# Attention's gates through DRAM: gating one token tile at a time instead of one column block of four tiles

## The chip, the cores and the metric

One core of one Trainium2 chip. The metric is the device time of one launch in microseconds (us), as the median of several runs. The engines are TensorE (PE; PEld is its weight load), VectorE (DVE), ScalarE (ACT), GpSimd (POOL) and the DMA queue that SyncE (SP) issues. [...]

## The reference, cut to what matters

Two layers over 1024 tokens of width 1024. In each layer one input projection feeds three groups of heads: sliding-window attention, retention and gated linear attention. Only the first is touched here.

```
s = einsum('bnqhgd,bnkhd->bnhgqk', qb, kk) * (D ** -0.5)      # 128 queries against 256 keys
p = softmax(concatenate([where(valid, s, -1e30), sink], -1))[..., :-1]
a_out = einsum('bnhgqk,bnkhd->bnqhgd', p, vv) * silu(ag)       # ag: the gate, a projection of h
y = concatenate([a_out, r_out, g_out], -1) @ w_out
x = x + gate * rms_norm(y, post_gain)
```

The attention has 8 query heads of width 64, two key heads, blocks of 128 tokens.

## The kernel before, in words

**Tiles.** The 1024 tokens are 8 tiles t of 128. Products that need full precision are made of two float32r halves: a tile is split into hi (a rounded copy) and lo (the rest), and three passes are summed, hi by hi, lo by hi, hi by lo (`PASSES`).

**Who sets the order.** The program is written as generators. `clk` is an estimate of PE's time that each matmul moves on; `job` puts a generator into a list, `pump` takes the jobs that are due forward between matmuls, a job says with `yield` how long it wants to wait (the table `L`, by names such as aq1 or ag1) or for which flag. So PE's order is the order in which matmuls are written under this clock, and it is kept. For the other engines and SP a scheduler orders the instructions when the kernel is built, by its own estimate of what is ready; a table `EN` picks the engine of many of them. Buffers are taken from pools by tag: `t2` is 10 buffers of 128x512, `t1` 7 of 128x256, `st` 5 for weights; PSUM has 8 banks, 3 for projections (`mm`) and 5 for the rest (`aux`).

**Attention.** `attn_run` starts one `attn_q` for each tile. A tile goes through these steps:
1. its queries are split into `qs` (hi on ACT, L841, lo on DVE, L842). `qs` has a tag of its own with one buffer;
2. 24 score matmuls into four `aux` banks (12 in tile 0 are smaller). Their first two use hi as weights, the next two lo;
3. ACT copies the previous block's scores out (L934, seen as L150 smx<-aux), DVE the current block's under a mask (L935), DVE takes the maximum (L937), ACT the eight exponentials with their sums (L940), DVE the reciprocal (L943), POOL the normalising product `pn` (L945), DVE the 32x32 transposes (L947), POOL four products `pr` that fix the window's edge (L956);
4. 80 small matmuls with the values (PV) into four `aux` banks, and four copies out into `ao`, alternately ACT and DVE (L978, seen as L150 and L152 t<-aux);
5. `ao` is stored to DRAM (`aoS`).

In PE's order the scores of tile t+1 stand before PV of tile t, with some 40 matmuls of the gates' projection (or of the output product) between each two.

**Gates.** In `layer`, for each half hf of the tokens (four tiles) and each of four column blocks k, `project_T` makes the gate of 128 columns by 512 tokens; the job `gate` (L1617) makes it silu-like (tanh on ACT, L1620, a product on DVE, L1621), keeps it in a `t2` buffer, and waits until all four tiles' attention is done. It then reads block k of the four tiles back from `aoS` (L1625), multiplies (L1627), splits the result (`mg` and `mgl`, both DVE, L1638 and L1639), and stores hi and lo to `mixS`, in the last layer also the whole to `mixF`. Only then do the four tiles' flags `mix1` come.

**After that.** The output product reads a tile's `mixS` (`load_mix`). The last layer works on pairs of tiles from tile 2 on (`Pair`): it reads both tiles' `mixF`, forms sums and differences on DVE (L1338 to L1341), and adds products up (L1378). Each of its product waits for one of three `mm` banks, which DVE or ACT must have read out. In layer 0 the next layer's normalisation (`pre`) follows each finished tile: DVE scales (L669), PE transposes.

Of the kernel before, what the change touches and what calls it, by code (L numbers as in the profile page):

```python
# [94 lines left out]
def trunk(ctx: ExitStack, tc: tile.TileContext, ins, cst, out):  # L95
# [88 lines left out]
    def lat(key, l):  # L184

        return L[key + "@1"] if l and key + "@1" in L else L[key]

# [3 lines left out]
    def flag(name, lat=0.0):  # L191
        flags[name] = clk[0] + lat
# [68 lines left out]
    mixF = dr.tile([NT, P, KT, P], F32, name="mixF")  # L261
    aoS = dr.tile([NT, P, 4, P], F32, name="aoS")
    vS = dr.tile([NT, P, P], F32, name="vS")
    sgS = dr.tile([NT, P, 256], F32, name="sgS")
    srS = dr.tile([NT, P, 256], F32, name="srS")
    tabS = dr.tile([NP_, P, 2, 256], F32, name="tabS")
# [573 lines left out]
    def split(hi, lo, src):  # L840
        A.activation(hi, src, AF.Copy)  # L841
        V.tensor_tensor(lo, src, f(hi), ALU.subtract)  # L842

    def attn_kv(l, t, pk):
        kr = t1()[:, 0:P]
        v = t1()[:, 0:P]
# [59 lines left out]

    def attn_q(l, t, q):

        qs = gp.tile([P, 2, 4, P], F32R, tag="qs", name=nm("qs"), bufs=1)
        split(qs[:, 0], qs[:, 1], q[:, :, P * (t % 4):P * (t % 4) + P])  # L910
        sm = gp.tile([P, 8, 129], F32, tag="smx", name=nm("smx"), bufs=SMB)
        V.tensor_copy(sm[:, :, 128], sink8[:, l])
        if t == 0:
# [5 lines left out]
        for g in range(2):  # L919
            for j in range(2):  # L920
                for i, (a, b) in enumerate(PASSES):
                    for r in range(2):
                        rr = slice(64 * r, 64 * r + 64)
                        mult(pss[g][r][:, j * n:(j + 1) * n], qs[rr, a, 2 * g + j], kv["kT"][b][rr, cols],
                             i == 0, i == 2, n / 4600.0)
        flag(("sc", l, t))
        if t % 4 == 3:
# [20 lines left out]
        cur, prev = kv[("v", t // 2)], kv.get(("v", max(t - 1, 0) // 2))  # L948
        tc_, tp = t % 2, (t - 1) % 2
        if t > 0:  # L950
            vd = gp.tile([P, P], F32, tag="vd", name=nm("vd"), bufs=1)
            G.tensor_tensor(vd, cur[:, 8 + tc_], prev[:, 8 + tp], ALU.subtract)
            pr = gp.tile([P, 8, 32], F32, tag="pr", name=nm("pr"), bufs=1)
            for i in range(4):
                rr = slice(32 * i, 32 * i + 32)
                eng(f"pr{i}").tensor_tensor(pr[rr], pb[rr, :, i, :], dmask[rr].unsqueeze(1).to_broadcast((32, 8, 32)),  # L956
                                            ALU.mult)
# [541 lines left out]
    def layer(l):  # L1499
# [111 lines left out]
        load(l, "ag0")  # L1611
        mx = {}

        def rows(d, hf, *i):
            return d[(slice(4 * hf, 4 * hf + 4), slice(None)) + i].rearrange("t p q -> p t q")

        def gate(g, hf, kk, pm):  # L1617
            k = 2 * g + kk
            th = t2()
            A.activation(th, pm, AF.Tanh, scale=0.5)  # L1620
            V.scalar_tensor_tensor(th, th, 1.0, pm, ALU.add, ALU.mult)  # L1621
            for t in range(4 * hf, 4 * hf + 4):
                yield (0.0, ("ao", l, t, g))
            ao = t2()
            dma("lao", ao.rearrange("p (t q) -> p t q", t=4), rows(aoS, hf, k))  # L1625
            yield lat("ag1", l)
            V.scalar_tensor_tensor(ao, th, 0.5, ao, ALU.mult, ALU.mult)  # L1627
            mh, ml = t2(F32R), t2(F32R)
            def tiles(x, ts):
                return x.rearrange("p (t q) -> p t q", t=4)[:, ts]  # L1630

            ts = slice(0, 4)
            if l == DEPTH - 1:
                t0 = max(PLAIN - 4 * hf, 0)
                if t0 < 4:
                    dma("sm0", rows(mixF, hf, k)[:, t0:4], tiles(ao, slice(t0, 4)))
                ts = slice(0, min(t0 + 1, 4)) if t0 else slice(0, 4, 2)
            copy("mg", tiles(mh, ts), tiles(ao, ts))  # L1638
            eng("mgl").tensor_tensor(tiles(ml, ts), tiles(ao, ts), tiles(f(mh), ts), ALU.subtract)  # L1639
            for a, m in ((0, mh), (1, ml)):  # L1640
                dma(f"sm{a}", rows(mixS, hf, a, k)[:, ts], tiles(f(m), ts))
# [65 lines left out]
        pump()  # L1707


B2, B1, BS, BST, MMB, SMB = 10, 7, 11, 5, 3, 3  # L1710
EN = {"shw0": "V", "shw1": "A", "shw2": "A", "shw3": "A", "slw0": "V", "slw1": "G", "slw2": "V", "slw3": "G", "sht2": "A", "sht3": "A", "sht4": "A", "slt2": "V", "slt3": "G", "slt4": "G", "sd": "V", "mh0": "A", "mh1": "A", "mh2": "A", "mh3": "A", "mf": "A", "ms0": "V", "ms1": "V", "ms2": "V", "ms3": "V", "yg0": "V", "yg1": "V", "ml0": "V", "ml1": "V", "ml2": "V", "ml3": "V", "mod0": "A", "mod1": "V", "qst": "S", "sv": "S", "lv": "S", "pr0": "G", "pr1": "G", "pr2": "G", "pr3": "G", "smh": "S", "sml": "S", "sm0": "S", "sm1": "S", "lao": "S", "sao": "S", "lmix": "S", "ssg": "S", "lsg": "S", "ssr": "S", "lsr": "S", "lx": "S", "sx": "A", "lw": "S", "lwm": "S", "whi0": "V", "whi1": "A", "whi2": "A", "whi3": "A", "wlo0": "V", "wlo1": "V", "wlo2": "V", "wlo3": "G", "xn0": "V", "xn1": "V", "hlo0": "V", "hlo1": "V", "rot0": "V", "rot1": "V", "rdec": "V", "kslo": "V", "qslo": "V", "vlo": "G", "kT": "A", "qT": "A", "sprev": "A", "pn": "G", "pf0": "A", "aoc0": "A", "aoc1": "V", "hng": "V", "mh": "A", "gso": "V", "mg": "V", "mgl": "V", "rT": "A", "rv": "A", "gv": "A", "gk": "A", "ak0": "V", "ak1": "V", "ak2": "V", "ak3": "V", "kd0": "G", "kd1": "G", "kd2": "G", "kx1": "G", "kx2": "G", "kx3": "V", "kx4": "V", "qb": "G", "stx": "V"}
L = {"sw1": 0.4, "ld1": 1.2, "ld2": 1.2, "ld1@1": 1.2, "ld2@1": 1.27, "swW00": 0.0, "swT1": 0.0, "swW11": 0.4, "swW10": 0.5, "tt1": 8.0, "tt2": 1.75, "tb1": 24.5, "tb2": 0.75, "pf3": 13.2, "pf1": 6.35, "pf2": 4.16, "mod1": 4.6, "mod2": 4.0, "mod3": 13.29, "mod4": 7.04, "mod5": 3.36, "mod6": 9.04, "pre1": 7.44, "kv1": 3.1, "kv2": 2.11, "aq1": 11.0, "aq7": 6.0, "ag1": 5.44, "aq2": 2.6, "aq6": 7.0, "aq3": 10.21, "aq4": 17.0, "aq5": 3.6, "hn1": 8.93, "hn2": 2.85, "gz1": 11.18, "gz2": 8.13, "gl1": 2.76, "gd3": 15.9, "gc1": 0.62, "gc2": 1.94, "gc3": 1.33, "gc4": 0.87, "gc6": 0.86, "gc5": 1.14, "rc1": 0.8, "rc2": 1.09, "rc3": 5.87, "rc4": 2.51, "fin1": 7.28, "lay1": 1.13, "gc4@1": 0.93, "mod2@1": 4.0, "mod3@1": 15.1, "mod5@1": 3.36, "mod6@1": 4.11, "pre1@1": 7.44, "kv1@1": 2.79, "kv2@1": 5.28, "aq1@1": 11.0, "aq7@1": 5.28, "ag1@1": 6.25, "aq2@1": 2.6, "aq6@1": 7.0, "aq3@1": 10.9, "aq4@1": 17.0, "aq5@1": 3.6, "hn1@1": 8.12, "hn2@1": 2.85, "gz1@1": 15.91, "gz2@1": 10.94, "gl1@1": 4.6, "gd3@1": 15.9, "gc1@1": 0.48, "gc2@1": 1.94, "gc3@1": 1.33, "gc6@1": 0.86, "gc5@1": 1.04, "rc1@1": 0.37, "rc2@1": 0.84, "rc3@1": 1.9, "rc4@1": 2.79, "fin1@1": 4.28, "lay1@1": 1.7}
CHUNK = 7
LAG = 2
FIN = 1
# [40 lines left out]
```

## Time and profile before

| | |
|---|---|
| runs, us | 1062.22, 1052.66, 1060.84; median 1060.84 |
| profiled execution, us | 1055.4, span 1053.6, mean granted clock 0.959 |
| PE busy | 968.1 us, 92% |
| PEld busy | 837.9 us, 80% |
| DVE busy | 703.8 us, 67% |
| ACT busy | 386.0 us, 37% |
| POOL busy | 259.7 us, 25% |
| DMA | 155.19 MB, mean 147 GB/s |
| attention's scores, layer 0 and layer 1 | from 328 to 437 us and from 830 to 944 us of the span |

Read the span as a queue of matmuls with holes. PE's order is fixed, so a hole is an instruction that waited, and the profile names what it waited for last. The holes' sizes are rows of the waits of PE and of PE's timeline (start, length, engine, line, operation, tile, count, and in brackets the idle time before it with its releaser); the other engines' timelines show why the releaser was late.

### The profile page before, as it was taken

What the parts mean: (1) busy time and instruction counts of PE and PEld (TensorE: products, weight loads), DVE (VectorE), ACT (ScalarE), POOL (GpSimd) and SP (SyncE); (2) the same over time, 40 slices, a digit from 0 to 9 for tenths busy, and PEclk for the clock granted to TensorE, in tenths of its full rate; (3) what the DMA queues carried; (4) which work ended last, traced back from release to release, by engine and by line L of the source; (5) the groups of instructions that cost most, each with busy time, mean ns of one, the idle gap of its engine ahead of it and who ended that gap; (6) DMA issues with size and microseconds to landing.
All of it is one profiled execution on the core that took longest, in us unless ns stands there. A gap on an engine that the chain in (4) does not pass through costs nothing. (4 is left out here: it accounts for less than half of the span.)

```text
span 1053.6 us, 21257 instructions
## 1 busy us (share of the span) xinstructions
PE 968.1 (92%) x7965; PEld 837.9 (80%) x7965; DVE 703.8 (67%) x1679; ACT 386.0 (37%) x1120; POOL 259.7 (25%) x306
## 2 busy tenths in 40 slices
PE   6899999998999997797989999999999998869696
PEld 1699999887988775686879999988888886657475
DVE  3889857677467877655486476756754676686666
ACT  2576312223314554413364431223331454443221
POOL 2332011322201334410123101123220135455001
PEclk8999999999999999899989999999989999969899
DMA  9744314333463435678534331451334242675874
GB/s 336 245 132 138 103 55 140 119 114 102 121 172 95 144 108 161 204 256 253 188 107 146 105 97 37 142 158 36 99 116 136 63 139 80 197 240 163 270 230 141
DMA packets 123335, 155.19 MB, mean 147 GB/s; under 512 B 12848, under 2 KB 72796, under 8 KB 123232
## 3 DMA queue, kind: packets, MB, share of 16 engines
q1 hardware_dynamic: 117536, 144.27, 43.7%
q10 hardware_dynamic: 5696, 9.56, 2.4%
q8 instruction: 63, 1.03, 0.4%
q14 instruction: 40, 0.33, 0.1%
HBM read 114.46 MB, written 37.22 MB: 144 GB/s over the span
## 5 line engine op out<-in xcount | busy, mean ns | idle before, releaser
L166 PE MATMUL mm<-arena 128*128 128x256 f32 (+2 forms) x1824 | 303.3, 323 | 2.1 <-ACT arena L707 1.8
L166 PE MATMUL mm<-arena,arena 128*128 128x256 f32 (+2 forms) x1824 | 296.6, 317 | 0.0
L166 PEld LDWEIGHTS mm<-arena 128*128 128x128 f32 x1824 | 262.3, 195 | 26.4 <-ACT arena L707 2.0
L166 PEld LDWEIGHTS mm<-arena,arena 128*128 128x128 f32 x1824 | 254.7, 190 | 23.6 <-issue 1.8
L166 PE MATMUL mm<-arena,mx 128*128 128x512 f32 (+1 forms) x564 | 137.3, 402 | 6.7 <-DVE t L1378 6.7
L638 POOL TENSOR_TENSOR sm<-sm,mhalf 128x1 f32<-128x1 f32 (+1 forms) x64 | 55.8, 872 | 353.9 <-DVE sm L637 350.2
L166 PEld LDWEIGHTS mm<-arena,mx 128*128 128x128 f32 x564 | 106.7, 197 | 32.4 <-DVE t L1378 5.4
L150 ACT ACTIVATE arena<-st 128x512 fp32r<-128x512 f32 x94 | 56.1, 628 | 78.6 <-PE mm L166 40.5
L536 POOL TENSOR_TENSOR arena<-st,arena 128x512 fp32r<-128x512 f32 x31 | 43.4, 1400 | 142.7 <-ACT arena L150 69.9
L181 PE MATMUL aux<-c_ident,t 128*128 128x128 f32 (+1 forms) x292 | 50.0, 290 | 22.2 <-DVE t L669 14.4
L940 ACT ACTIVATE smx<-smx,sm 128x129 f32<-128x129 f32 x128 | 49.7, 391 | 31.4 <-DVE sm L937 31.4
L536 DVE TENSOR_TENSOR arena<-st,arena 128x512 fp32r<-128x512 f32 x77 | 58.1, 775 | 3.5 <-ACT arena L150 1.7
L181 PEld LDWEIGHTS aux<-c_ident,t 128*128 128x128 f32 (+1 forms) x292 | 35.8, 147 | 30.6 <-DVE t L669 11.0
L166 PE MATMUL aux<-kT,qs 64*128 64x256 f32 (+1 forms) x384 | 33.6, 311 | 27.9 <-DVE t L152 15.8
L150 ACT ACTIVATE t<-aux 128x128 f32<-128x128 f32 (+3 forms) x92 | 32.4, 379 | 70.5 <-PE aux L181 51.5
L367 DVE SCALAR_TENSOR_TENSOR acc<-st,c_act,acc 128x512 f32<-128x512 f32 x60 | 45.5, 758 | 15.4 <-DMA st<-in_w_mod_dram 14.8
L166 PEld LDWEIGHTS aux<-kT,qs 64*128 64x128 f32 x384 | 27.7, 204 | 35.2 <-DVE t L152 17.4
L945 POOL TENSOR_TENSOR smx<-smx,sm 128x1024 f32<-128x1024 f32 x16 | 31.2, 1949 | 98.7 <-DVE sm L943 85.8
L956 POOL TENSOR_TENSOR pr<-smx,c_dmask 32x256 f32<-32x256 f32 x56 | 45.3, 809 | 12.2 <-DVE smx L947 4.5
L166 PEld LDWEIGHTS aux<-t,mx 32*128 32x128 f32 (+1 forms) x896 | 40.9, 194 | 4.0 <-issue 3.0
L166 PE MATMUL aux<-t,mx 32*128 32x32 f32 (+1 forms) x896 | 42.1, 279 | 0.0
L1281 DVE SCALAR_TENSOR_TENSOR t<-t,sm,t 128x512 f32<-128x512 f32 x32 | 24.2, 781 | 26.6 <-DMA t<-in_x_dram 15.0
(225 smaller groups left out, 1359.4 us busy)
## 6 DMA issues: line engine op xcount, KB each, us to landing
st<-in_w_in_dram SPq DMA_DIRECT2D x96, 256.0 KB, 4.2
st<-in_w_mod_dram SPq DMA_DIRECT2D x64, 256.0 KB, 3.0
mx<-mixS SPq DMA_DIRECT2D x20, 512.0 KB, 4.6
mixS<-t SPq DMA_DIRECT2D x72, 128.0 KB, 2.6
st<-in_w_last_dram SPq DMA_DIRECT2D x36, 256.0 KB, 3.5
wm<-in_w_mod_dram SPq DMA_DIRECT2D x12, 512.0 KB, 5.3
t<-in_x_dram SPq DMA_DIRECT2D x24, 256.0 KB, 4.5
vx<-vS SPq DMA_DIRECT2D x40, 128.0 KB, 2.4
```

The lines of the kernel that those rows point to most:

```text
L150: A.activation(dst, src, AF.Copy)
L166: T.matmul(dst, lhsT, rhs, start=start, stop=stop)
L181: T.transpose(dst, src, idn)
L367: V.scalar_tensor_tensor(acc, wt, c_act[:, k:k + 1], acc, ALU.mult, ALU.add)
L536: e.tensor_tensor(lo, st, f(hi), ALU.subtract)
L638: G.tensor_tensor(r, r, mhalf[:, :w], ALU.pow)
L940: A.activation(sm[:, h, :], sm[:, h, :], AF.Exp, bias=mx[:, h:h + 1], accum_out=sums[:, h:h + 1])
L945: eng("pn").tensor_tensor(ph, ph, rs.unsqueeze(2).to_broadcast((P, 8, P)), ALU.mult)
L956: eng(f"pr{i}").tensor_tensor(pr[rr], pb[rr, :, i, :], dmask[rr].unsqueeze(1).to_broadcast((32, 8, 32)), ALU.mult)
L1281: V.scalar_tensor_tensor(xt[j], yg[j], r, xt[j], ALU.mult, ALU.add)
```

## The change

It has four parts.

1. **Gates to DRAM.** `gate` is no job any more. It stores its 128x512 result to a new DRAM tensor `gS` and sets a flag; nothing waits in it.
2. **Gating by tile.** `attn_q` goes on after its store: it waits for the four gate flags of its half, reads the tile's `ao` and its gates back (two DMAs of 256 KB, each partition's 2 KB in one piece), multiplies them (L994 of the changed kernel), stores the whole in the last layer's tiles from 2 on, splits (except the last layer's odd tiles from 3 on), stores hi and lo, and sets the tile's four `mix1` flags.
3. **Buffers.** The split queries come from the shared `t2` pool, two buffers a tile, instead of one buffer `qs`. The values `v` get a tag of their own (`va`, two buffers), `vd` and `pr` two buffers instead of one, `t1` eight instead of seven.
4. **Engines and clock.** The queries' lo half (`qsl`, L913) and the gated tile's lo half (`mgl`, L1001) go from DVE to POOL, all four copies of PV's result to ACT. `aq1` goes from 11.0 to 12.0 in layer 0, `aq2` from 2.6 to 3.2 in both, `ag2` is new with 3.0.

```
-        qs = gp.tile([P, 2, 4, P], F32R, tag="qs", name=nm("qs"), bufs=1)
-        split(qs[:, 0], qs[:, 1], q[:, :, P * (t % 4):P * (t % 4) + P])
+        qs = [t2(F32R).rearrange("p (k q) -> p k q", k=4) for _ in range(2)]
+        qt = q[:, :, P * (t % 4):P * (t % 4) + P]
+        A.activation(qs[0], qt, AF.Copy)
+        eng("qsl").tensor_tensor(qs[1], qt, f(qs[0]), ALU.subtract)
...
-        for g in range(2):
-            flag(("ao", l, t, g), lat("aq5", l))
+        yield lat("aq5", l)
+        for k in range(4):
+            yield (0.0, ("g", l, t // 4, k))
+        ao, gt = t2(), t2()
+        av = ao.rearrange("p (k q) -> p k q", k=4)
+        for d, src in ((av, aoS), (gt.rearrange("p (k q) -> p k q", k=4), gS)):
+            dma("lao", d, src[t])
+        yield lat("ag1", l)
+        V.scalar_tensor_tensor(ao, gt, 0.5, ao, ALU.mult, ALU.mult)
+        whole = l == DEPTH - 1 and t >= PLAIN
+        if whole:
+            dma("sm0", mixF[t, :, 0:4, :], av)
+        if not whole or t % 2 == 0:
+            mh, ml = t2(F32R), t2(F32R)
+            copy("mg", mh, ao)
+            eng("mgl").tensor_tensor(ml, ao, f(mh), ALU.subtract)
+            for a, m in ((0, mh), (1, ml)):
+                dma(f"sm{a}", mixS[t, :, a, 0:4, :], f(m).rearrange("p (k q) -> p k q", k=4))
+        for k in range(4):
+            flag(("mix1", l, t, k), lat("lay1", l))
...
         def gate(g, hf, kk, pm):
             k = 2 * g + kk
             th = t2()
             A.activation(th, pm, AF.Tanh, scale=0.5)
             V.scalar_tensor_tensor(th, th, 1.0, pm, ALU.add, ALU.mult)
-            for t in range(4 * hf, 4 * hf + 4):
-                yield (0.0, ("ao", l, t, g))
-            ao = t2()
-            dma("lao", ao.rearrange("p (t q) -> p t q", t=4), rows(aoS, hf, k))
-            yield lat("ag1", l)
-            V.scalar_tensor_tensor(ao, th, 0.5, ao, ALU.mult, ALU.mult)
...
-            for t in range(4 * hf, 4 * hf + 4):
-                flag(("mix1", l, t, k), lat("lay1", l))
+            dma("sg", gS[4 * hf:4 * hf + 4, :, k].rearrange("t p q -> p t q"), th.rearrange("p (t q) -> p t q", t=4))
+            flag(("g", l, hf, k), lat("ag2", l))
...
-                    job(gate(g, hf, kk, pm))
+                    gate(g, hf, kk, pm)
```

The built programs differ in order as follows. POOL's order in layer 0 from tile 2's `pn` on (W is the lo half of a weight block; the tile's number stands behind the name; the scheduler's memset and `vd` products are kept):

```
before: pn2 vd2 pr2 pn3 vd3 pr3 W pn4 W vd4 pr4 W pn5 vd5 pr5 pn6 memset vd6 pr6 memset pn7 vd7 pr7
after:  pn2 pr2 vd3 qsl3 pn3 pr3 qsl4 W vd4 pn4 W pr4 vd5 qsl5 mgl0 mgl1 mgl2 W mgl3 pn5 pr5 qsl6 vd6
        memset vd7 pn6 qsl7 mgl4 pr6 memset mgl5 pn7 pr7
```

In layer 1 the changed order ends `pn6 W pr6 W vd7 qsl7 W W mgl4 pn7 pr7`. On ACT, the hi half of tile t+1's queries stood before tile t's exponentials and now stands behind them and behind PV's first copy of tile t-1. On PE the scores stand up to 8 matmuls later or earlier among the same others; in layer 0 the last 24 gate matmuls stood between the scores of tiles 6 and 7 and now stand before the scores of tile 6, so that only PV of tile 5 is left between the two. DVE and SP follow: DVE's product with the gates and its cast come once a tile instead of four times after tiles 3 and 7.

More of the change, by code (lines that the diff above doesn't have):

```diff
@@ L263, in trunk @@
     vS = dr.tile([NT, P, P], F32, name="vS")
+    gS = dr.tile([NT, P, 4, P], F32, name="gS")
     sgS = dr.tile([NT, P, 256], F32, name="sgS")
@@ L845, in attn_kv @@
         kr = t1()[:, 0:P]
-        v = t1()[:, 0:P]
+        v = gp.tile([P, P], F32, tag="va", name=nm("va"), bufs=2)
         i = A.activation(v, pk[:, 128:256], AF.Copy)
@@ L950, in attn_q @@
         if t > 0:
-            vd = gp.tile([P, P], F32, tag="vd", name=nm("vd"), bufs=1)
+            vd = gp.tile([P, P], F32, tag="vd", name=nm("vd"), bufs=2)
             G.tensor_tensor(vd, cur[:, 8 + tc_], prev[:, 8 + tp], ALU.subtract)
-            pr = gp.tile([P, 8, 32], F32, tag="pr", name=nm("pr"), bufs=1)
+            pr = gp.tile([P, 8, 32], F32, tag="pr", name=nm("pr"), bufs=2)
             for i in range(4):
@@ L1612, in layer @@
         mx = {}
-        def rows(d, hf, *i):
-            return d[(slice(4 * hf, 4 * hf + 4), slice(None)) + i].rearrange("t p q -> p t q")
         def gate(g, hf, kk, pm):
@@ L1621, in gate @@
             V.scalar_tensor_tensor(th, th, 1.0, pm, ALU.add, ALU.mult)
-            for t in range(4 * hf, 4 * hf + 4):
-                yield (0.0, ("ao", l, t, g))
-            ao = t2()
-            dma("lao", ao.rearrange("p (t q) -> p t q", t=4), rows(aoS, hf, k))
-            yield lat("ag1", l)
[L1627 to L1641, printed above, removed]
-            for t in range(4 * hf, 4 * hf + 4):
-                flag(("mix1", l, t, k), lat("lay1", l))
+            dma("sg", gS[4 * hf:4 * hf + 4, :, k].rearrange("t p q -> p t q"), th.rearrange("p (t q) -> p t q", t=4))
+            flag(("g", l, hf, k), lat("ag2", l))
         for g in range(2):
@@ L1712 @@
[L1712 removed]
+B2, B1, BS, BST, MMB, SMB = 10, 8, 11, 5, 3, 3
```

6 lines of the change are left out of this document (3 added, 3 removed).

## The prediction

> **What bounds the kernel now.** I read the busy shares first, then the busy time in windows, then the waits of PE, then the timelines around the holes that they name.
>
> ```profile
> PE 968.1 (92%) x7965; PEld 837.9 (80%) x7965; DVE 703.8 (67%) x1679; ACT 386.0 (37%) x1120; POOL 259.7 (25%) x306
> ```
>
> PE is busy for 968.1 of 1053.6 us and its order is fixed, so the change can only remove or add holes, or slow the clock. The windows (length, then busy time of PE, PEld, DVE, ACT and POOL with counts, the granted clock, the DMA share, GB/s) show where holes lie:
>
> ```profile
> 400.00:450.00 50.00, 39.70 (x413) 31.29 (x414) 32.98 (x61) 19.04 (x74) 21.47 (x24) 0.90 0.59 179
> 900.00:950.00 50.00, 37.64 (x327) 29.31 (x326) 38.38 (x63) 23.15 (x83) 23.23 (x23) 0.80 0.71 220
> 950.00:1000.00 50.00, 39.86 (x309) 30.78 (x309) 31.11 (x55) 12.14 (x29) 14.72 (x13) 0.95 0.66 211
> ```
>
> In the late part of attention (first two rows) and behind layer 1's attention (third) PE stands still for 10 to 12 us in 50, and in attention POOL's share (43% and 46%) is well above its mean of 25%. The waits of PE from 830 us on (total idle, number, longest) and of layer 0's stretch name the releasers:
>
> ```profile
> PE aux L166 <- DVE t L152: 8.1, 4, 2.5
> PE aux L181 <- DVE t L669: 5.3, 1, 5.3
> ...
> PE aux L166 <- DVE t L152: 7.7, 3, 4.4
> PE mm L166 <- DVE t L1378: 6.7, 3, 5.0
> PE mm L166 <- DVE t L1340: 4.2, 2, 3.8
> ```
>
> So there are two kinds. In attention, scores wait for banks that PV's copies must empty. Behind attention, three long holes stand where DVE comes late. The change touches both.
>
> **Attention, layer 0.** PE's timeline gives the ends of the scores of tiles 2 to 7, POOL's the normalising products and the ends of `pr`:
>
> ```profile
> 353.34 1.68 PE L166 MATMUL aux<-kT,qs 64*128 64x256 f32 x24
> 371.46 0.98 PE L166 MATMUL aux<-kT,qs 64*128 64x256 f32 x12 [2.54 <-DVE t L152]
> 383.77 1.68 PE L166 MATMUL aux<-kT,qs 64*128 64x256 f32 x24
> 400.95 1.37 PE L166 MATMUL aux<-kT,qs 64*128 64x256 f32 x12 [2.16 <-DVE t L152]
> 435.58 1.65 PE L166 MATMUL aux<-kT,qs 64*128 64x256 f32 x12 [1.53 <-DVE t L152]
> ```
>
> ```profile
> 364.86 2.36 POOL L945 TENSOR_TENSOR smx<-smx,sm 128x1024 f32<-128x1024 f32 x1 [6.51 <-DVE sm L292]
> 369.42 3.30 POOL L956 TENSOR_TENSOR pr<-smx,c_dmask 32x256 f32<-32x256 f32 x4 [1.79 <-DVE smx L947]
> 379.14 1.90 POOL L945 TENSOR_TENSOR smx<-smx,sm 128x1024 f32<-128x1024 f32 x1 [6.42 <-DVE sm L282]
> 382.39 3.12 POOL L956 TENSOR_TENSOR pr<-smx,c_dmask 32x256 f32<-32x256 f32 x4 [0.94 <-DVE smx L912]
> 399.66 2.53 POOL L956 TENSOR_TENSOR pr<-smx,c_dmask 32x256 f32<-32x256 f32 x3
> 419.81 4.08 POOL L956 TENSOR_TENSOR pr<-smx,c_dmask 32x256 f32<-32x256 f32 x4 [0.92 <-DVE smx L947]
> ```
>
> From the end of a tile's scores to the end of its `pr`, which I call C, tiles 2 to 5 took 372.72-355.02 = 17.7, 385.51-372.44 = 13.1, 402.19-385.45 = 16.7 and 423.89-402.32 = 21.6 us, in the mean 17.3. From scores 2 to scores 7 went 437.23-355.02 = 82.2 us, five loops of 16.4.
>
> Before, scores t+1 didn't wait for `pr` of tile t: the lo half of the queries was DVE's. Now it is POOL's, and POOL's built order has it behind `pr` of the tile before for scores 3 to 6. A score group's third matmul needs it. So a loop is C, plus POOL's lo operation, plus 22 of the 24 score matmuls (22/24 of the first row's 1.68 us, 1.5). The lo operation has the shape of the lo half of a weight block:
>
> ```profile
> L536 POOL TENSOR_TENSOR arena<-st,arena 128x512 fp32r<-128x512 f32 x31 | 43.4, 1400 | 142.7 <-ACT arena L150 69.9 <-ACT qs L841 59.6 <-issue 5.5
> L842 DVE TENSOR_TENSOR qs<-mx,qs 128x512 fp32r<-128x512 f32 x16 | 12.0, 748 | 1.0 <-ACT qs L841 1.0
> L152 DVE COPY t<-aux 128x128 f32<-128x128 f32 x32 | 7.6, 274 | 0.0
> L150 ACT ACTIVATE t<-aux 128x128 f32<-128x128 f32 x32 | 7.1, 265 | 8.2 <-PE aux L166 4.8 <-DVE t L1281 3.4
> L1627 DVE SCALAR_TENSOR_TENSOR t<-t,t 128x512 f32<-128x512 f32 x16 | 11.8, 744 | 16.7 <-DMA t<-aoS 16.7
> L1639 DVE TENSOR_TENSOR t<-t,t 128x512 fp32r<-128x512 f32 x8 | 5.8, 725 | 0.8 <-DMA mixS<-t 0.6
> ```
>
> A loop is then C + 1.4 + 1.5 = C + 2.9. What PE has to do between two score groups, some 44 gate matmuls, PV and the scores, is shorter (a stretch of that kind was 371.46 to 385.45, 14.0 us, holes in it), so this chain would set the loop's length.
>
> C should shrink, since DVE and ACT, late in order, make it long. Its floor is tile 3's 13.1 less the 0.69 us that one L842 took from DVE in it, 12.4; its ceiling is the old mean of 17.3. Tile 5's 21.6 holds the old gating burst on DVE:
>
> ```profile
> 373.69 0.69 DVE L842 TENSOR_TENSOR qs<-mx,qs 128x512 fp32r<-128x512 f32 x1
> 407.96 2.21 DVE L1627 SCALAR_TENSOR_TENSOR t<-t,t 128x512 f32<-128x512 f32 x2 [2.89 <-DMA t<-aoS]
> 469.56 0.69 DVE L1627 SCALAR_TENSOR_TENSOR t<-t,t 128x512 f32<-128x512 f32 x1 [5.69 <-DMA t<-aoS]
> ```
>
> The burst leaves it; but three `mgl` of 1.4 us each now stand ahead of `pn` of tile 5 on POOL, 4.2 us, free only where `pn` would have waited longer than that (6.51 and 6.42 us in two rows above). I take C = 15.0, about the middle.
>
> The last loop, 6 to 7, has `qsl` behind `pn` alone. Tile 3's way from scores to the end of `pn` was 379.14+1.90-372.44 = 8.6; with 2.9 that is 11.5. Scores 2 come 8 gate matmuls later (about 2.0: 8 of the 44 that stand in the 11.3 us from 372.44 to 383.77) and behind `vd` (0.5, an estimate: 128 elements a partition against the 256 of one `pr` operation, 0.8). So 4 x 17.9 + 11.5 + 2.5 = 85.6 against 82.2: **+3.4 us**.
>
> **Attention, layer 1.**
>
> ```profile
> 856.37 1.68 PE L166 MATMUL aux<-kT,qs 64*128 64x256 f32 x24
> 937.30 2.96 POOL L567 TENSOR_TENSOR arena<-st,arena 128x512 fp32r<-128x512 f32 x2
> 941.92 1.65 PE L166 MATMUL aux<-kT,qs 64*128 64x256 f32 x11 [1.51 <-DVE t L152]
> ```
>
> Five loops took 943.57-858.05 = 85.5. After: four loops of 17.9, and a last one in which `qsl` stands behind two weight halves (2 x 1.5, second row), `pr` and `vd`: 13.1 + 3.0 + 0.5 + 2.9 = 19.5. Together 91.1: **+5.6 us**.
>
> **The holes behind attention.**
>
> ```profile
> 487.11 1.08 PE L181 MATMUL aux<-c_ident,t 128*128 128x128 f32 x4 [5.30 <-DVE t L669]
> 983.70 2.96 PE L166 MATMUL mm<-arena,mx 128*128 128x512 f32 x12
> 990.88 0.69 DVE L1378 TENSOR_TENSOR t<-mm,kept 128x512 f32<-128x512 f32 x1 [1.63 <-DMA mixF<-t]
> 991.62 4.61 PE L166 MATMUL mm<-arena,mx 128*128 128x512 f32 x12 [4.96 <-DVE t L1378]
> 996.86 0.69 DVE L1338 TENSOR_TENSOR t<-t,t 128x512 f32<-128x512 f32 x1 [4.50 <-DMA t<-mixF]
> 1000.01 5.46 PE L166 MATMUL mm<-arena,a 128*128 128x512 f32 x12 [3.79 <-DVE t L1340]
> ```
>
> The 5.30 at 487.11 stands behind a normalisation that DVE reached late: since its L1627 waited for the read-back (5.69 idle at 469.56) the four products, casts and lo halves came as one burst. In layer 1 DVE waits at 990.88 for a store to free its buffer and at 996.86 for pairs that were stored late, and PE stands still 4.96 and 3.79. Both holes cost twice: twelve matmuls that take 2.96 us took 4.61 and 5.46 behind them, 1.65 + 2.50 = 4.15 more.
>
> After, only tile 7's gating is left at the end of a half: one product, one cast, one read-back, with `mgl` on POOL; tiles 4 to 6 are done in attention. One L1627 of 0.74 us in place of a burst of four with their L1639 of 0.73. If that removes all, the gain is 5.3 + 4.96 + 3.79 + 4.15 = **-18.2**. Its bounds are 0 (a tile's way gets longer by a store of its gates and a POOL operation, so tile 7 may be as late as before) and -18.2. I take it whole, since these holes' DVE waits are the burst's own.
>
> [...]
>
> **The rest, at nothing.** DVE loses 16 x 0.75 (L842), some 13 x 0.73 (`mgl`) and 32 x 0.27 (copies), about 30 us; POOL gains 29 x 1.4 = 41 us on 259.7. ACT gains 32 x 0.27. Four copies in a row on ACT end 0.5 us later than two and two; PV's banks are then still free long before `qsl` in a loop of 17.9, which hides it; without that cover it is 0.5 x 14 = 7. SP issues 80 DMAs for gating instead of 56; what stands behind a waiting read-back in SP's order are weight loads and the stores of other tiles. They are hidden while PE has weights ahead; if not, one read-back's wait like the 5.69 above in each layer, +11. A gain from DVE's free 30 us outside attention I bound by 0 to -2, since PE's holes there are few.
>
> [...]
>
> ```profile
> 365.38 1.85 DVE L293 SCALAR_TENSOR_TENSOR mod<-sm,sm 128x4 f32<-128x4 f32 x1
> ```
>
> This 128x4 operation took 1.85 us, ending at 367.23, as `pn` ended at 364.86+2.36 = 367.22. [...]
>
> **Sum.** +3.4 + 5.6 - 18.2 = -9.2. The profiled execution took 1055.4 (span 1053.6), so 1046.2 on its terms. That execution lies between the runs shown (1052.66, 1060.84, 1062.22); the mean of the four is 1058.3, and 1058.3 - 9.2 = **1049**, my forecast.
>
> **Rivals.** All are on the same 1058.3.
>
> *POOL sets the loops and the end (slower).* `qsl`, `mgl` and `pr` stand in one line on POOL. If C keeps its 17.3, eight loops are 2.3 longer than I take, +18.4; the same lateness puts `mgl` of the last tiles behind weight halves and keeps half of the tail holes, +9.1. That gives 1049 + 27.5 = 1076.5. It decides from C of about 16.5 on. For it: the order on POOL, and 21.47 busy us in 50 there already. Against it: DVE's relief in each loop.
>
> *No change.* The tail holes go by half (-9.1), attention gives +9.0: 1058. For it: tile 7's chain is as long as ever, and the last pairs need it.
>
> *More gain.* C falls to tile 3's 13.1: eight loops of 16.0, -15.2, so 1034. For it: tile 3 is the undisturbed tile, and the burst and L842 have gone. Against it: `mgl` ahead of `pn`.
>
> *It doesn't do what it says.* The gating is still bunched because all read-backs wait for the last gate column; then tails remain wholly, 1067. The built order of layer 0 (`mgl` 0 to 2 ahead of `pn5`) speaks against it; I count it with the first.
>
> **Chances.** Forecast 0.36 (1043 to 1055), more gain 0.20, no change 0.10, slower 0.34, wide because C's price is a choice between 12.4 and 17.3. One per cent, 10.6 us, is about the spread of the three runs (9.6), and what a measurement can tell from no change. Faster by more: 0.20 and 0.22 of the forecast's 0.36, 0.42. Within: 0.14 + 0.10 + 0.02, 0.26. Slower: 0.32. The range goes from the gain rival's 1034 to a little above the slow one's, 1078; the forecast's own is 1043 to 1055.
>
> **What would show it.** Right: in POOL's timeline the lo half of the queries comes straight behind `pr`, PE's third score matmul waits for it and no longer for L152; loops of about 18 us; the holes of 5.30, 4.96 and 3.79 gone, and no x12 above 3 us near 990. Wrong: loops below 16 (C was sized too long) or above 19; a new wait of PE for weights (SP held up) or for tile 7's `mixS`; DVE operations stretched beside POOL's; or a changed duration of PE outside attention, which I put at nothing.

## The result, and the profile after

| | before | changed |
|---|---|---|
| median of 20 runs each, us | 1059.49 | 1052.20 |
| lowest to highest, us | 1052.66 to 1067.36 | 1048.30 to 1057.92 |
| profiled execution, us | 1055.4, span 1053.6 | 1055.04, span 1052.9 |

The ratio is 0.994, with a 95% interval of 0.9919 to 0.996. The change gains 7.3 us: faster, by less than one per cent. The forecast of 1049 us lies 3.2 us below the median. The profiled execution of the changed kernel lies 2.8 us above its median and that of the kernel before 4.1 us below its own, so the spans of the two profiles compared below differ by 0.7 us only. The other 6.6 us of the gain stand in no stage below: there is one profile of each kernel.

The page of the changed kernel, busy time by engine:

```profile
PE 964.2 (92%) x7965; PEld 836.5 (79%) x7965; DVE 689.4 (65%) x1612; ACT 389.8 (37%) x1152; POOL 298.2 (28%) x335
```

POOL took 38.5 us more, as worked out (41). The waits of PE (total idle, number, longest), first for the stretch of layer 0's attention, then from 830 us on:

```profile
PE aux L166 <- POOL t L913: 15.8, 5, 4.9
PE aux L166 <- ACT t L912: 8.1, 2, 4.5
...
PE aux L166 <- POOL t L913: 21.7, 5, 6.8
PE mm L166 <- DVE t L1399: 6.8, 2, 6.7
PE aux L166 <- ACT t L912: 5.7, 2, 4.8
```

L913 is the queries' lo half, L912 their hi half. They have taken the place of PV's copies (L152 and L150) as what scores wait for; with 51.3 us together they cost PE more than the copies did (27.8 us by the same two views of the kernel before: 15.8 for L152, 12.0 for L150). In PE's timeline of the changed kernel, all scores of tiles 2 to 7 of layer 0, the first product of layer 1, scores 2 and 7 of layer 1, and the holes:

```profile
350.82 1.70 PE L166 MATMUL aux<-kT,t 64*128 64x256 f32 x24
370.47 2.71 PE L166 MATMUL aux<-kT,t 64*128 64x256 f32 x22 [4.66 <-POOL t L913]
387.32 1.58 PE L166 MATMUL aux<-kT,t 64*128 64x256 f32 x22 [0.56 <-POOL t L913]
410.33 2.72 PE L166 MATMUL aux<-kT,t 64*128 64x256 f32 x22 [3.86 <-POOL t L913]
432.84 2.72 PE L166 MATMUL aux<-kT,t 64*128 64x256 f32 x22 [4.88 <-POOL t L913]
444.88 2.72 PE L166 MATMUL aux<-kT,t 64*128 64x256 f32 x22 [1.80 <-POOL t L913]
552.66 7.54 PE L166 MATMUL mm<-arena,arena 128*128 128x272 f32 x59
850.16 1.70 PE L166 MATMUL aux<-kT,t 64*128 64x256 f32 x24
887.27 2.35 PE L166 MATMUL aux<-kT,t 64*128 64x256 f32 x22 [2.09 <-POOL t L913]
905.08 2.72 PE L166 MATMUL aux<-kT,t 64*128 64x256 f32 x22 [2.45 <-POOL t L913]
947.29 2.72 PE L166 MATMUL aux<-kT,t 64*128 64x256 f32 x22 [4.18 <-POOL t L913]
989.91 4.69 PE L166 MATMUL mm<-arena,mx 128*128 128x512 f32 x12 [6.67 <-DVE t L1399]
```

The scores' ends cut each execution into stages that hold the same work, up to eight matmuls. I use them for every kernel: ahead of attention (to the end of scores 2, and from the first 128x272 product of layer 1 to the end of its scores 2), attention (end of scores 2 to end of scores 7), behind it (from there to layer 1's first product, and to the span's end). The table is worked out from such rows of each profile, each stage rounded before it is added. It shows one execution per kernel: e7 and e9 differ only in the engine of the gated lo half and still lie 4.0 us apart ahead of attention, so differences of that size between two rows are not to be read; and e4's profile is the slowest of its ten runs (1073.87 us, median 1066.40). In the kernel before, layer 1's first product stands at this row:

```profile
551.20 7.91 PE L166 MATMUL mm<-arena,arena 128*128 128x272 f32 x62
```

| us | ahead, layers 0 + 1 | attention 0, 1 | behind 0, 1 |
|---|---|---|---|
| before | 355.0 + 306.8 = 661.8 | 82.2, 85.5 | 114.0, 110.0 |
| changed | 352.5 + 299.2 = 651.7 | 95.1, 98.1 | 105.1, 102.9 |
| e1_lo_on_dve | 649.7 | 88.5, 94.1 | 108.4, 99.8 |
| e2_buffers_alone | 646.6 | 91.1, 94.6 | 115.7, 107.0 |
| e3_gates_alone | 661.8 | 80.2, 80.2 | 115.1, 103.8 |
| e4_fewer_buffers | 669.1 | 94.8, 96.3 | 108.9, 102.9 |
| e5_shared_twelve | 665.8 | 89.7, 92.3 | 113.8, 100.4 |
| e6_own_hi | 648.6 | 87.7, 86.1 | 114.9, 103.1 |
| e7_moved_engines | 661.1 | 75.1, 74.4 | 117.5, 104.4 |
| e8_own_queries_and_buffers | 654.7 | 82.1, 85.2 | 116.6, 105.1 |
| e9_copies_on_act | 665.1 | 73.8, 74.9 | 116.1, 104.6 |
| e10_t1_eight | 652.2 | 75.0, 76.3 | 118.3, 103.7 |
| e11_values_apart | 670.9 | 75.1, 75.2 | 117.4, 103.2 |
| e12_own_queries_lo_on_pool | 652.7 | 73.7, 78.7 | 118.6, 101.5 |

So the small change of the time is three large ones: attention +25.5, behind it -16.0, ahead of it -10.1; together -0.6.

### The profile page after: what moved, and what is told of

It is laid out like the page before. It is cut to its first block, busy times and chain, and to the rows that moved or that the text cites. A ratio compares the mean times of both kernels' runs of the same rounds, so it can differ in the third digit from the quotient of the medians.

```text
span 1052.9 us, 21298 instructions
## 1 busy us (share of the span) xinstructions
PE 964.2 (92%) x7965; PEld 836.5 (79%) x7965; DVE 689.4 (65%) x1612; ACT 389.8 (37%) x1152; POOL 298.2 (28%) x335
## 3 DMA queue, kind: packets, MB, share of 16 engines
q8 instruction: 63, 1.03, 0.4%
## 4 chain that ended last, share of the span: by engine, by line
PE 61%; DVE 12%; DMA 10%; POOL 7%; issue 5%; ACT 3%; SPq 1%; ACTq 0%; POOLq 0%; DVEq 0%
PE mm L166 47%; PE aux L166 11%; PE aux L181 3%; DMA st<-in_w_in_dram 2%; POOL pr L959 2%; ACT smx L943 1%; POOL sm L639 1%; POOL smx L948 1%; DMA st<-in_w_out_dram 1%; DMA xk<-in_x_dram 1%; POOL t L913 1%; SPq L155 1%; DVE arena L537 1%; DMA t<-xs 1%; DMA t<-in_x_dram 1%
## 5 line engine op out<-in xcount | busy, mean ns | idle before, releaser
L166 PE MATMUL mm<-arena 128*128 128x256 f32 (+2 forms) x1824 | 299.6, 321 | 2.1 <-ACT arena L708 1.8
L166 PEld LDWEIGHTS mm<-arena,mx 128*128 128x128 f32 x564 | 104.4, 194 | 35.4 <-ACT mx L150 7.1
L166 PE MATMUL aux<-kT,t 64*128 64x256 f32 (+1 forms) x384 | 39.8, 363 | 51.3 <-POOL t L913 37.5
L150 ACT ACTIVATE arena<-st 128x512 fp32r<-128x512 f32 x94 | 55.9, 629 | 69.3 <-PE mm L166 34.2
L166 PEld LDWEIGHTS aux<-kT,t 64*128 64x128 f32 x384 | 33.7, 256 | 59.3 <-POOL t L913 39.7
L150 ACT ACTIVATE t<-aux 128x128 f32<-128x128 f32 (+3 forms) x124 | 38.6, 356 | 73.0 <-PE aux L181 63.2
L368 DVE SCALAR_TENSOR_TENSOR acc<-st,c_act,acc 128x512 f32<-128x512 f32 x60 | 47.2, 787 | 18.1 <-DMA st<-in_w_mod_dram 17.4
L959 POOL TENSOR_TENSOR pr<-smx,c_dmask 32x256 f32<-32x256 f32 x56 | 47.6, 850 | 14.9 <-DVE smx L950 7.6
L181 PEld LDWEIGHTS aux<-c_ident,t 128*128 128x128 f32 (+1 forms) x292 | 35.3, 145 | 15.2 <-DVE t L670 8.4
L938 DVE COPY_PREDICATED smx<-c_curmask,aux 128x256 f32<-128x256 int32 x64 | 24.4, 444 | 30.6 <-ACT smx L150 30.6
L702 ACT ACTIVATE t<-aux,mod,mod 128x128 f32<-128x128 f32 x68 | 25.8, 459 | 41.6 <-PE aux L181 14.8
```

Source lines behind the costliest of these rows:

```text
L150: A.activation(dst, src, AF.Copy)
L166: T.matmul(dst, lhsT, rhs, start=start, stop=stop)
L181: T.transpose(dst, src, idn)
L368: V.scalar_tensor_tensor(acc, wt, c_act[:, k:k + 1], acc, ALU.mult, ALU.add)
L702: A.activation(hf[:, ks], at[kt], AF.Identity, scale=gain, bias=shift)
L938: V.copy_predicated(sv, curmask.unsqueeze(1).to_broadcast((P, 2, P)), pv[:, :, n // P - 1, :])
```

## The experiments

Each median stands with its ratio to the kernel before on the same chip and the 95% interval. In the edits B1 and B2 are the numbers of `t1` and `t2` buffers; in the table of engines "V" is DVE, "A" ACT and "G" POOL; `qsl` is the queries' lo half, `mgl` the gated tile's lo half, `aoc1` every second copy of PV's result. "Values apart" means the values in their own two buffers (`va`). No run tries the second buffers of `vd` and `pr` or the clock entries (`aq1`, `aq2`, `ag2`) alone.

**e1_lo_on_dve.** From the changed kernel:

```
-"qsl": "G"
+"qsl": "V"
```

> The changed kernel with the queries' lo half on DVE again; all else as changed. Theory A (attention pays for the lo half on POOL): PE's waits for POOL L913 (37.5 us, 10 times, in the changed kernel's profile) go; from scores 2 to scores 7 it falls from 95.1 and 98.2 us back towards the 82.2 and 85.5 of before, so 15 to 25 us less: 1027 to 1037 us. Rival B (POOL was only the last of several late things; the hi half on ACT, now behind a tile's exponentials, waits as long): PE's waits for ACT L912 (13.8 us) grow in its place and less than 8 us are gained: 1045 to 1052 us.

1040.27 us, ratio 0.9816 (0.9776 to 0.9856). In between: attention falls by 10.6 us to 182.6, not to the 167.7 of before. The waits of PE in its layer 0, from 350 to 450 us, show that the place changed and not the chain:

```profile
PE aux L166 <- DVE t L913: 10.1, 4, 4.0
PE aux L166 <- ACT t L912: 8.6, 2, 4.6
```

The lo half is late on DVE too, and the hi half before it.

**e2_buffers_alone.** From the kernel before:

```
-        qs = gp.tile([P, 2, 4, P], F32R, tag="qs", name=nm("qs"), bufs=1)
+        qs = [t2(F32R).rearrange("p (k q) -> p k q", k=4) for _ in range(2)]
-        v = t1()[:, 0:P]
+        v = gp.tile([P, P], F32, tag="va", name=nm("va"), bufs=2)
-B1 7, vd and pr bufs=1
+B1 8, vd and pr bufs=2
```

> The kernel before with the buffers of the change alone: split queries in the shared 128x512 buffers, values in a tag of their own, vd and pr two buffers, t1 eight; gates, engines and clock entries as before, the lo half on DVE. Theory A (the buffers give the gain ahead of attention, about 7 us in layer 0 and 10 us in layer 1, where PE waited for the recurrences' tiles and its clock fell): those stretches get as short as in the changed kernel, and attention stays as it was: 1040 to 1048 us. Rival B (that gain comes from DVE's freed 30 us, or is only a disturbance of the one profiled execution): within 0.4% of before, 1055 to 1063 us. Rival C: the shared buffers make the queries late, attention gets longer by more than the gain, above 1063 us.

1059.40 us, ratio 0.9994 (0.9966 to 1.0021). By its time this is rival B; by its stages A's gain ahead of attention (-15.2) and C's longer attention (+18.0) both come and nearly cancel. Without any change to the gates, and with the lo half on DVE, sharing the queries' buffers lengthens attention.

**e3_gates_alone.** From the changed kernel: the queries' own buffer, values in t1, B1 7, `vd` and `pr` one buffer; `qsl`, `mgl` and `aoc1` on "V"; aq1 11.0, aq2 2.6.

> The changed kernel with buffers, engines and clock entries as before (own single buffer for the split queries, values in t1, t1 seven, vd and pr one, lo half, gated lo half and every second copy on DVE; aq1 11.0, aq2 2.6): gates through DRAM and gating by tile alone. Theory A (gating by tile empties the holes behind attention and costs little inside it): the stretch from the end of scores 7 to layer 1's first projection 5 to 9 us shorter, the end 7 to 13 us shorter, attention within 4 us: 1038 to 1050 us. Rival B (the tile's products, casts and lo halves on DVE within attention make its loops longer by what is saved behind it): 1054 to 1066 us.

1046.47 us, ratio 0.9885 (0.9827 to 0.9943). The total lies in theory A's range, its stages do not: in layer 1 attention is 5.3 us shorter (A: within 4) and the end 6.2 shorter (A: 7 to 13); in layer 0 attention is 2.0 shorter and the stretch behind it 1.1 longer instead of 5 to 9 shorter. Nearly all of the gain is in layer 1.

**e4_fewer_buffers.** From the changed kernel:

```
-        v = gp.tile([P, P], F32, tag="va", name=nm("va"), bufs=2)
+        v = t1()[:, 0:P]
-B1 8
+B1 7
```

> The changed kernel with the values in t1 again and t1 seven buffers. Theory A (these buffers give the gain ahead of attention): the stretches ahead of attention are long again by 7 and 10 us: 1066 to 1072 us. Rival B (they do nothing there; DVE's relief does it): within 0.4% of the changed kernel, 1048 to 1056 us.

1066.40 us, ratio 1.006 (1.0038 to 1.0083). Ahead of attention +17.4 in the profile, which lies 7.5 us above its median, attention unchanged within 2.1; at the medians 14.2 us more than the changed kernel: theory A. Without these buffers the change would have been a small loss.

**e5_shared_twelve.** From e3_gates_alone:

```
-        qs in a buffer of their own (4 KB a partition), B2 10
+        qs = [t2(F32R).rearrange("p (k q) -> p k q", k=4) for _ in range(2)], B2 12
```

> Gates through DRAM and gating by tile alone (the run in which everything else was as before), but the split queries come from the shared 128x512 buffers, and those get the room: 12 instead of 10. Same room, same engines. Theory A (a shared buffer is claimed in the order of the program, so the queries of tile t+1 come behind the copies of PV's result of tile t-1 on ACT, and with them behind the exponentials of tile t; the number of buffers doesn't matter): attention from 80.2 and 80.2 us to 88 to 97 us in each layer, 1060 to 1078 us. Rival B (the changed kernel has too few shared buffers, and the queries wait for a store that frees one): with 12 attention stays within 3 us of 80.2 in each layer, 1043 to 1052 us.

1064.10 us, ratio 1.0058 (1.003 to 1.0086). Theory A: attention 182.0 against 160.4, +21.6, with the same room and the same engines. Two more shared buffers don't bring the queries forward. On ACT the hi half of tile t+1 runs behind the exponentials of tile t and next to the first copy of PV of tile t-1, with 12 buffers here as with 10 in e2: exponentials from 381.28, first copy at 386.76 and hi half at 386.94 us here, 372.04, 378.10 and 378.32 us there.

**e6_own_hi.** From e3_gates_alone: the hi half in a buffer of its own, the lo half in a shared one, values apart, B1 8.

> Gates through DRAM and gating by tile with the room of the split queries divided: a buffer of their own for the hi half, the lo half (on DVE) from the shared ones, t1 eight, values in a tag of their own; vd, pr, engines and clock entries as before. In the built order the hi half stands early again and the lo half behind the transposes of the tile before. Theory A (either half is enough to make the scores late): ahead of attention 355 and 304 us or less become 350 and 299, attention 85 to 92 us a layer, 1045 to 1055 us. Rival B (only the hi half on ACT counts): attention about 80 a layer and the buffers' gain ahead of it: 1034 to 1042 us.

1042.80 us, ratio 0.9847 (0.98 to 0.9894), attention 87.7 and 86.1: A as to the stages, the time between the two, since the gain ahead of attention (-13.2) came with it. In layer 0's attention, from 350 to 450 us, PE waits for nothing but the lo half:

```profile
PE aux L166 <- DVE t L913: 17.6, 4, 8.0
```

**e7_moved_engines.** From e3_gates_alone:

```
-"mgl": "V", "aoc1": "V"
+"mgl": "G", "aoc1": "A"
```

> Gates through DRAM and gating by tile alone, with the gated lo half on POOL and all four copies of PV's result on ACT as in the changed kernel; queries and buffers as before. Theory A (these two moves cost next to nothing, the queries' sharing and their lo half on POOL make up all of attention's 25.5 us): attention within 3 us of 80.2 in each layer, 1042 to 1051 us. Rival B (POOL, with the gated lo halves ahead of the normalising product, and ACT, with four copies in a row, are part of it): attention 84 to 90 us a layer, 1053 to 1065 us.

1037.48 us, ratio 0.9797 (0.9742 to 0.9851). Neither theory: attention does not stay, it gets 10.9 us shorter.

**e8_own_queries_and_buffers.** From e3_gates_alone: values apart, B1 8, and four staging buffers for weights instead of five.

> Gates through DRAM and gating by tile, the queries in their own buffer, and the room for t1 eight and the values' own two buffers taken from the weights' staging (four buffers instead of five). Theory A (the gains are independent: tile gating, and the buffers ahead of attention): ahead of attention 5 to 10 us less than the gates alone, attention 80 us a layer: 1034 to 1042 us, the best so far. Rival B (four staging buffers make weights late, PE waits for the conversion of a weight block): 1050 to 1070 us.

1046.72 us, ratio 0.9888 (0.9852 to 0.9923). Not decided: ahead of attention -7.1, but attention +6.9; several things were changed at once. B's reason does not show: in attention PE waits for PV's copies as in e3 (28.9 us against 24.1, from 350 to 450 and from 830 to 940 us) and for no weight block. Why attention is longer stays open.

**e9_copies_on_act.** From e3_gates_alone: `aoc1` to "A" alone.

> Gates through DRAM and gating by tile alone, with all four copies of PV's result on ACT; the gated lo half stays on DVE. The run that also had the lo half on POOL took 75.1 and 74.4 us for attention against 80.2 and 80.2 without both. Theory A (the waits for DVE L152 were those of a busy DVE, and the copies' move takes them away): attention 74 to 77 us a layer, 1036 to 1041 us. Rival B (it was the gated lo half that left DVE): attention 79 to 81 us, 1044 to 1049 us.

1036.36 us, ratio 0.9789 (0.9735 to 0.9843), attention 73.8 and 74.9. Theory A: the copies' move alone takes 11.7 us out of attention; the gated lo half on POOL adds nothing to it. PE's 16.4 us of waits for L152 in e3 are gone; waits for the copies on ACT (L150) remain, 21.5 us over the span against 12.1.

**e10_t1_eight and e11_values_apart.** From e7_moved_engines, the first two lines in both, then one of the others:

```
-        b = gp.tile([P, 256], F32, tag="tr", name=nm("tr"), bufs=1)
+        b = t1()
+B1 8                                                    (e10)
+        v = gp.tile([P, P], F32, tag="va", ..., bufs=2) (e11)
```

> Gates through DRAM, gating by tile, gated lo half on POOL, all copies of PV's result on ACT, the queries in their own buffer and their lo half on DVE, and t1 eight buffers; the room for it comes from the rotation's scratch tile, which is now one of t1's. The values stay in t1. Theory A (it is the number of t1 buffers that frees the recurrences ahead of attention): the stretches ahead of attention 354.6 and 306.5 us become 349 to 352 and 298 to 301 us; attention stays at 75: 1024 to 1032 us. Rival B (the values' own tag does it): those stretches stay, 1036 to 1042 us.

> As the run with t1 eight, but the room goes to two buffers of their own for the values, and t1 stays seven. Theory A (the values sit in t1 until they are stored, and hold its buffers): the stretches ahead of attention become 349 to 352 and 298 to 301 us: 1024 to 1032 us. Rival B (the number of t1 buffers does it): those stretches stay, 1036 to 1042 us.

1027.13 us, ratio 0.9695 (0.9655 to 0.9736), and 1043.81 us, ratio 0.9851 (0.9796 to 0.9905). It is the number of t1 buffers: ahead of attention 652.2 against 670.9. (With the scratch tile in t1 and only seven buffers, e11 is 9.8 us longer there than e7.) e10 beats both kernels, by 32 us and 25 us at the medians.

**e12_own_queries_lo_on_pool.** From e10_t1_eight:

```
-"qsl": "V"
+"qsl": "G"
```

> The run with t1 eight, with the queries' lo half on POOL as in the changed kernel, but the queries still in their own buffer. In the built order POOL then makes the lo half of tile t+1 ahead of the normalising product of tile t, not behind its edge products. Theory A (the lo half on POOL costs attention some 10 us, as between the changed kernel and the one with the lo half on DVE, for POOL is slower and busier): attention 79 to 83 us a layer, 1035 to 1045 us. Rival B (it was only the place behind the edge products, which came with the shared buffers, that cost): attention 73 to 78 us a layer, 1022 to 1031 us.

1027.31 us, ratio 0.9707 (0.9661 to 0.9752): rival B (layer 1's attention, 78.7, lies a little above its 73 to 78). It is the same as e10 as far as these runs can tell: by the two intervals, a difference of less than some 6 us would not show. POOL's timeline in it, around tile 5 of layer 0:

```profile
404.41 1.28 POOL L914 TENSOR_TENSOR qs<-mx,qs 128x512 fp32r<-128x512 f32 x1
408.55 1.90 POOL L949 TENSOR_TENSOR smx<-smx,sm 128x1024 f32<-128x1024 f32 x1 [2.86 <-DVE sm L947]
415.90 2.97 POOL L960 TENSOR_TENSOR pr<-smx,c_dmask 32x256 f32<-32x256 f32 x4
418.95 1.31 POOL L914 TENSOR_TENSOR qs<-mx,qs 128x512 fp32r<-128x512 f32 x1
```

The first lo half here (tile 6's) stands ahead of the normalising product of tile 5, in time that POOL had idle (2.86 us behind it). The lo half on POOL costs nothing that these runs can tell where its queries come early.

## Why the prediction was right or wrong

**The time came out right by luck, from terms that were not.** Forecast: attention +9.0, behind it -18.2, the rest 0, sum -9.2. Measured in the profiles: +25.5, -16.0, -10.1, sum -0.6; at the medians -7.3. Attention cost 16.5 us more than forecast, and most of that was made up by 10.1 us ahead of attention, a stage that I had put at nothing. The profiles alone would have missed the forecast sum by 8.6 us; that the medians come within 1.9 us of it is no merit of the terms. (The base has a slip: the mean of the four times is 1057.8, not 1058.3; the forecast would still round to 1049.)

Of my own signs of being right two came: scores wait for L913 and no longer for L152, and the holes of 5.30, 4.96 and 3.79 are gone. Two did not: the first four loops of layer 0 took 20.7, 15.7, 24.2 and 22.5 us instead of about 18, and twelve matmuls near 990 took 4.69. Of the signs of being wrong two came: loops above 19, and a changed time outside attention.

**Attention: the chain was right, its terms were too small.** The prediction's step was a loop of C + 1.4 + 1.5. POOL's rows of the changed kernel for tiles 2 to 5 of layer 0 (the last `pr` row is preceded by `pn` as before):

```profile
365.42 3.25 POOL L959 TENSOR_TENSOR pr<-smx,c_dmask 32x256 f32<-32x256 f32 x4 [1.36 <-DVE smx L950]
382.49 3.10 POOL L959 TENSOR_TENSOR pr<-smx,c_dmask 32x256 f32<-32x256 f32 x4 [1.36 <-DVE smx L915]
404.12 4.35 POOL L959 TENSOR_TENSOR pr<-smx,c_dmask 32x256 f32<-32x256 f32 x4
408.55 0.51 POOL L955 TENSOR_TENSOR vd<-vx 128x128 f32<-128x128 f32 x1
409.02 1.26 POOL L913 TENSOR_TENSOR t<-mx,t 128x512 fp32r<-128x512 f32 x1
428.57 2.88 POOL L959 TENSOR_TENSOR pr<-smx,c_dmask 32x256 f32<-32x256 f32 x4 [1.36 <-DVE smx L915]
```

C was 368.67-352.52 = 16.1, 385.59-373.18 = 12.4, 408.47-388.90 = 19.6 and 431.45-413.05 = 18.4, mean 16.6 against the 15.0 that I took and the 12.4 to 17.3 that bounded it. Loop 4 to 5 follows the formula to a tenth: 19.6 + 0.5 (`vd`) + 1.3 (lo) + 2.7 (22 matmuls) = 24.1, measured 413.05-388.90 = 24.2. The 22 matmuls are the other mis-sized term: 2.7 us and not 1.5 behind almost every hole, 1.58 only behind the one of 0.56. I had seen the slow matmuls behind the old tail holes and did not price them behind the new ones. The four loops from scores 2 to scores 6 took 83.0 us (435.56-352.52) against 71.6; four times 1.6 for C and three times 1.2 for slow score groups make 10.0 of the 11.4. The last loop took 12.0 as forecast (11.5), without the 2.5 that I had added for a later start, so 95.1 stands against 85.6. In layer 1 it was 98.1 against 91.1.

Part of C comes from a wait that I put at nothing. DVE's rows of the changed kernel at tile 4:

```profile
397.44 0.75 DVE L368 SCALAR_TENSOR_TENSOR acc<-st,c_act,acc 128x512 f32<-128x512 f32 x1 [3.84 <-DMA st<-in_w_mod_dram]
399.22 0.69 DVE L994 SCALAR_TENSOR_TENSOR t<-t,t 128x512 f32<-128x512 f32 x1 [1.03 <-DMA t<-gS]
399.83 0.20 DVE L946 RECIPROCAL sm<-sm 128x8 f32<-128x8 f32 x1
401.72 1.17 DVE L994 SCALAR_TENSOR_TENSOR t<-t,t 128x512 f32<-128x512 f32 x1 [1.14 <-DMA t<-gS]
402.81 1.23 DVE L950 STREAM_TRANSPOSE smx<-smx 128x1024 f32<-128x1024 f32 x1
```

Tile 4's exponentials ended at 396.84 (ACT), but its reciprocal came only at 399.83: DVE stood first at a product that waited for a weight block (L368), then at the gating product of an earlier tile, which waited 1.03 us for the read-back of its gates and took 0.69. The normalising product on POOL ended at 402.34 and the transposes began at 402.81, behind another gating product. So the gating on DVE put about 1.7 + 0.5 us into this C of 19.6; its second wait, 1.14 us, passed while POOL was at the normalising product and cost nothing here. `pr` itself took 4.35 us instead of 2.9 to 3.3 in the other rows; why is open.

**What the step overlooked: why the lo half stood there at all.** I took the order on POOL for a property of the move to POOL. e5 and e12 separate the two. Sharing the buffers with the lo half on DVE costs 21.6 us (e3 to e5); the lo half on POOL with its own buffer costs nothing that these runs can tell (e10 to e12). Only where both meet does POOL's part cost 10.6 us (e1 to the changed kernel). ACT's rows show the difference in the kernel before and the changed one, each after scores 3 (which ended at 372.44 and 373.18):

```profile
373.02 0.63 ACT L841 ACTIVATE qs<-mx 128x512 fp32r<-128x512 f32 x1
```

```profile
378.44 0.39 ACT L943 ACTIVATE smx<-smx,sm 128x129 f32<-128x129 f32 x1
381.62 0.28 ACT L150 ACTIVATE t<-aux 128x128 f32<-128x128 f32 x1 [1.67 <-PE aux L166]
381.81 0.63 ACT L912 ACTIVATE t<-mx 128x512 fp32r<-128x512 f32 x1
```

With its own buffer the next tile's hi half is made 0.6 us after the scores; from shared ones 8.6 us after them, behind the exponentials and behind the first copy of PV's result, which itself takes a shared buffer. That this copy's claim on the shared buffers holds the order is argued from the built order, which more buffers did not change; no run isolates it.

**The copies.** I priced their move to ACT at nothing, or +7 without cover; it was wrong in sign: -11.7 us of attention (e9), as PE no longer waits for L152. That those waits were long because DVE was busy is likely and not shown. In the changed kernel the move gains nothing that one can see, since its scores wait for the queries.

**Ahead of attention.** I bounded it by 0 to -2 and took 0; it was -10.1. Where t1 has seven buffers the stage took 661 to 671 us, with eight 647 to 655, in all fourteen kernels. The waits of DVE and ACT in the kernel before, from 700 to 830 us, name what held the `t1` buffers, stores to DRAM; L847 takes a buffer for the values, L999 one for another group's result:

```profile
ACT t L847 <- DMA mixF<-t: 4.5, 2, 2.4
DVE t L999 <- DMA mixS<-t: 3.1, 2, 1.9
```

PE itself waited little there, 5.2 us in layer 1's stage against 2.0 in the changed kernel, of 7.6 that it lost. That those waits lead back to the buffers is argued; that the number of buffers counts is shown (e4; e10 against e7 and e11). The windows of the kernel before, then of the changed one, show a price beyond the waits: the granted clock falls to 0.75 and 0.91 in two stretches (the number behind POOL's count), and is 1.00 in the changed kernel.

```profile
760.00:780.00 20.00, 19.52 (x177) 18.81 (x178) 8.28 (x31) 6.21 (x19) 4.33 (x7) 0.75 0.31 97
780.00:800.00 20.00, 18.56 (x206) 16.45 (x205) 9.90 (x32) 4.61 (x19) 3.85 (x5) 0.91 0.47 139
```

```profile
760.00:780.00 20.00, 19.89 (x272) 18.89 (x272) 13.63 (x43) 8.46 (x28) 7.15 (x10) 1.00 0.40 123
780.00:800.00 20.00, 20.00 (x206) 17.52 (x203) 9.38 (x36) 4.06 (x17) 2.53 (x4) 1.00 0.44 130
```

The matmuls show it too: before the hole of 1.81 us at 760.48, 15 of 128x256 took 1.96 us (754.80), behind it 7 took 1.84 (760.82). I counted PE's idle time and not the slow matmuls behind it, the same omission as in attention.

**Behind attention.** -16.0 against -18.2, but that these holes' waits were the burst's own holds only in part: with tile gating alone (e3) the two stretches are 5.1 us shorter. The holes of 5.30, 4.96 and 3.79 are gone; in layer 1 one of 6.67 came in their place (989.91 above, with twelve matmuls of 4.69 behind it), so that layer 1 gave 7.1 and not 12.9. PE waits there for an addition that DVE reaches only at 989.08, behind tile 7's gating product, which waited 2.36 us for its gates (978.70), and the pairs' sums and differences: tile 7 is late, as the lower bound of this term had it. In e3 a hole of 4.5 us stands at the same addition. In layer 0 the shorter stretch is partly the longer attention's: from the end of scores 2 to layer 1's first product it was 196.2 before, 200.2 in the changed kernel and 195.3 with tile gating alone. Tile gating alone empties nothing behind attention in layer 0: PE waited 8.9 us there before and 8.8 in e3, of which 3.6 in one hole of the same normalisation and 4.1 for the read-back of the gated result. e10 is the same; from 450 to 560 us:

```profile
PE mm L166 <- DMA mx<-mixS: 8.1, 2, 6.9
PE aux L181 <- DVE t L670: 5.1, 2, 3.6
```

**The rivals.** The first one, POOL setting the loops, described attention's size (+27.4 by its sum, C above 16.5, three loops above 19) and not the end, and by e1 POOL was only part of the cause; "more gain" named what e10 and e12 reach by another way.

## What to carry to other kernels

Before two uses share a rotating pool, ask what else claims a buffer between them: an instruction that was free to run early may then be ordered behind the others' claims. Here a faster engine won back 10.6 of 25.5 us (e1), and two more buffers did not bring it forward (e5). Cost a hole as its length plus the slow matmuls that may follow it, also where single waits are near two microseconds (behind waits of 2.09 and 2.45 us 22 score matmuls took 2.35 and 2.72 us, behind one of 0.56 us 1.58). And when a change has several parts, a time that hardly moves may hide large opposite terms; cut the trace into stages with equal work before believing any one cause.

## What the runs showed of the hardware

The clock fell behind holes shorter than those that I had looked at (4.96 and 3.79 us): 22 score matmuls took 2.72 us behind a hole of 2.45 us and 2.35 behind one of 2.09, against 1.58 behind 0.56 (rows of the changed kernel in the first section). The granted clock over these stretches was 0.50 (905.1 to 907.7), 0.60 (887.3 to 889.6) and 1.00 (387.3 to 388.9). The length alone does not decide it: in the kernel before, the twelve score matmuls behind the hole of 2.54 us took 0.98 us at a clock of 1.00 (371.46), those behind the hole of 2.16 took 1.37 at 0.63 (400.95). Both rows stand in the prediction, where I did not compare them.

POOL ran in the built orders listed with the change: its rows of layer 0's attention stand in them in both profiles (364.86 to 449.62 us in the kernel before, 361.70 to 465.18 us in the changed one). On DVE a wait held up what stood behind it: tile 4's reciprocal came 2.99 us after its exponentials had ended, behind a product that waited 3.84 us for a weight block and one that waited 1.03 us for the gates (the DVE rows of the changed kernel above).

Sixteen operations moved from DVE to POOL changed nothing that these runs can tell (e10, 1027.13 us; e12, 1027.31 us; less than some 6 us would not show), though they took POOL 21.4 us in e12 and DVE 12.5 us in e10. The 128x4 operation of 1.85 us that the prediction shows beside POOL took 0.16 us at its other place (L293 at 299.15 us of the kernel before); no run shows why. The lo half itself took these times on POOL in the changed kernel and on DVE in e10:

```profile
L913 POOL TENSOR_TENSOR t<-mx,t 128x512 fp32r<-128x512 f32 x16 | 21.2, 1326 | 48.4 <-DMA vS<-va 25.0 <-ACT t L912 23.0
```

```profile
L914 DVE TENSOR_TENSOR qs<-mx,qs 128x512 fp32r<-128x512 f32 x16 | 12.5, 781 | 1.5 <-ACT qs L913 1.5
```
